# Mixture-of-experts stage: w1 and w3 side by side in the array's columns, and another order of the expert steps

## The chip, the cores and the metric

The kernel runs on one core of a Trainium2 chip. The metric is the device time of one launch in microseconds (us). PE is TensorE's matmul pipe and PEld its weight load, DVE is VectorE, ACT is ScalarE, SP is the engine whose queue issues the weight loads. Line numbers (L1541) are those of the kernel before.

## The reference, cut to what matters

A hybrid layer is followed by a two-layer block. The second layer of that block ends in a mixture of eight experts: 256 tokens of width 1024, each sent to its two best experts, each expert a gated feed-forward of inner width 3584.

```
def moe_swiglu(x, w_router, w1, w3, w2):
    ...
    top_vals, top_idx = lax.top_k(logits, TOP_K)          # TOP_K = 2
    gates = jax.nn.softmax(top_vals, axis=-1)
    ...
    def block_fn(args):
        tok, e = args
        xb = xf[tok]
        return (jax.nn.silu(xb @ w1[e]) * (xb @ w3[e])) @ w2[e]
    ...
h = layer_norm(DEEPNORM_ALPHA * h + f + e, ln2_g[i], ln2_b[i])
```

All is float32. Everything ahead of the experts (some 1000 us) is untouched by the change.

## The kernel before, in words

The experts are sorted at run time by how many tokens they have (`who`), so that "expert 1" below is a rank and not a number of the model. Expert 0 is always the model's first one. Each rank has room for a fixed number of tokens: 64 for 0, 4 and 5, 128 for 2 and 3, 128 + 64 for 1 (its second block has the number `NE`), 32 for 6 and 7. A block of 128 is "wide" and a block of 64 or 32 "narrow". Five more passes for experts that overflow stand in a conditional at the end and are not run on these inputs.

The inner width is cut into NJ = 7 slices of 512, and one slice of one expert is a step: 56 steps, listed in `STEPS`. A step reads six units of 1 MiB: w1 as two units (input rows 0 to 511 and 512 to 1023), w3 as two, w2 as two (output columns 0 to 511 and 512 to 1023). `_moe_order` gives the order of the units: the four of a step's w1 and w3, then the two of w2 of the step before. `prepare` issues a unit's load on SP's queue into the next of a ring of raw buffers (eight of them from step 2 on) and, for ranks in `WIDE`, has ACT cast each half to a high part (`whi`, L302) and DVE subtract to a low part (`wlo`, L303). `rows_unit` runs three units ahead of their use, so these instructions stand in the queues of SP, ACT and DVE ahead of what belongs to the units in use.

`hidden` is the up part of a step (x w1 and x w3). A wide block keeps the tokens transposed and split in two (`xg`) and takes three matmuls for each 128 rows of a unit (`mm3`, L321 to L323, 128 columns of the array). A narrow block (`xn`) takes the raw float32 weights (L1584; each float32 product appears as two instructions) and only 64 or 32 columns of the array; `pair` puts neighbouring k into different column groups, so that two (64) or four (32) of them run side by side, and their partial sums stand in different partitions of one PSUM bank. `turned` transposes such a bank (L1568) and DVE adds the partial sums (L1572). This is done twice for a narrow block in each step: for w1 in the middle of the up part and for w3 in `later`. `later` also applies silu and the product, and for a wide block transposes it (L1553). `down` is the product with w2, for the step before; `passes` puts `later` between its two halves. Ranks in `aside` add each step's product to a tile in SBUF (L1604); the others accumulate in two PSUM banks over all seven steps. After an expert's last step `scaled` and `scatter` (L1626) add its tokens to the residual.

`gather` (L1430 and on) picks a group's tokens by a one-hot matmul, for whole groups of ranks, up to three steps ahead of their first use. `last_sums` and `last_norm` end the kernel after the last step.

The order of the instructions on each engine comes from a scheduler that runs when the kernel is built: it takes the written order as priority and gives buffers to tiles as they come free.

```
STEPS = _steps((0, 0, 0, 4, 0, 4, 0, 4, 0, 4, 0, 4, 4, 4) + (1, 5, 6) * NJ + (2, 7) * NJ + (3,) * NJ)
```

Of the kernel before, what the change touches and what calls it, by code (L numbers as in the profile page):

```python
# [8 lines left out]
F32 = mybir.dt.float32  # L9
# [4 lines left out]
OP = mybir.AluOpType  # L14
# [192 lines left out]

def _moe_order(steps):

    out = []  # L210
    for i in range(len(steps) + 1):
        if i < len(steps):
            out += [(steps[i][0], 6 * steps[i][1] + t) for t in range(4)]
        if i:
            out += [(steps[i - 1][0], 6 * steps[i - 1][1] + t) for t in (4, 5)]
    return out

STEPS = _steps((0, 0, 0, 4, 0, 4, 0, 4, 0, 4, 0, 4, 4, 4) + (1, 5, 6) * NJ + (2, 7) * NJ + (3,) * NJ)  # L220

WIDE = (1, 2, 3)

# [22 lines left out]
class Kern:  # L246
# [925 lines left out]
    def moe(self, l, h, hT, out):  # L1172
# [6 lines left out]
        with ExitStack() as ctx:  # L1179
# [143 lines left out]
            def widen():  # L1323
                rctx.close()
                more = ctx.enter_context(tc.tile_pool(name="more", bufs=1, side="right"))
                self.xgs = [more] * 4
                self.xns = [more] * 3 + self.xns
                self.ohs = [more] * 4 + self.ohs
                self.ya = more
            es = [nc.sync.value_load(who[0:1, i:i + 1], min_val=0, max_val=NE - 1) for i in range(1, NE)]  # L1330
            self.srcs += [(A["wm"][0, u] if e == 0 else self.wsrc(es[e - 1], u), e in WIDE)
# [4 lines left out]
            def rows():  # L1336

                for i in range(2):
                    t = self.ya.tile([P, D], F32, name=f"y{5 + i}")
                    for c in range(2):  # L1340
                        acc = self.bank([P, 4, P], "acc")
                        for k in range(4):
                            at = KD * i + 4 * c + k
                            mm(acc[:, k], self.gb[:, at:at + 1].to_broadcast([P, P]), self.ident, start=True, stop=True)
                        nc.scalar.copy(t[:, 512 * c:512 * c + 512], acc.rearrange("p a b -> p (a b)"))
                    gb.append(t)
                fin.extend(self.ya.tile([P, D], F32, name=n) for n in ("y7", "y8"))
                stats.append(self.mp.tile([P, NT, 2, 6], F32, name="stats"))

            def done(sums):  # L1350
                self.last_norm(r, sums, fin, stats[0], *gb, out)
            self.passes(posp, gatep, STEPS, r, first, [
                {4: [(4, b)]}, {1: [(1, a), (NE, b)], 5: [(5, b)]},
                {6: [(6, q)], 7: [(7, q)]}, {2: [(2, a)]}, {3: [(3, a)]}], (NE, 4, 5, 6, 7), {2: narrow, 3: widen, len(STEPS) - NJ + 2: rows}, done)
            n = nc.values_load(who[0:1, NE + MORE:], min_val=0, max_val=MORE)
            with ExitStack() as some:
                for i in range(MORE):
                    some.enter_context(tc.If(n > i))
                    e = nc.sync.value_load(who[0:1, NE + i:NE + i + 1], min_val=0, max_val=NE - 1)
                    steps = _steps((0,) * NJ)  # L1360
                    self.srcs, self.ready = [(self.wsrc(e, u),) for _, u in _moe_order(steps)], []
                    self.passes(posp, gatep, steps, r, {}, [{0: [(NE + 1 + i, a)]}], done=done)

    def last_norm(self, x, sums, out, st, g, b, dst):

# [47 lines left out]
    def gather(self, gate, group, oh):  # L1413
# [5 lines left out]
        blocks = sum(group.values(), [])  # L1419
        starts = [sum(n for _, n in blocks[:i]) for i in range(len(blocks) + 1)]  # L1420
        width = starts[-1]
        gsl = self.gat.tile([P, 3], F32, name="gsl", bufs=2)
        xs = [tuple(self.turn_of(self.xgs, [P, KD, P], "xg") for _ in range(2)) if n == P else
              (self.turn_of(self.xns, [P, KD, n], "xn", F32),) for _, n in blocks]
        for k in range(0, KD, 2):
# [31 lines left out]
    def passes(self, pos, gate, steps, r, got, groups, aside=(), events={}, done=None):  # L1457

        todo, left, ys = None, None, {}
        groups = list(groups)  # L1460
        for i, step in enumerate(steps + [None]):
            new = None
            if i in events:
                events[i]()

            for e, _ in steps[i:i + (3 if i > 5 else 1)]:
                if e not in got:
                    got.update(self.gather(gate, groups[0], self.one_hot(pos, groups.pop(0))))
            later = None
            if step:  # L1470
                e, j = step
                out, later = self.hidden([b[1] for b in got[e]])
                new = (e, j, out)
            if left:
                self.scatter(left, r)
                left = None
            if not step:
                break
            if todo:
                e, j, gs = todo  # L1480
                if j == 0:
                    ys[e] = [self.ya.tile([P, D], F32, name=f"y{7 if b[0] == 4 else b[0]}") if b[0] in aside else
                             [self.bank([P, 512], "sm") for _ in range(2)] for b in got[e]]
                    ys[e] = [[y[:, :512], y[:, 512:]] if b[0] in aside else y for y, b in zip(ys[e], got[e])]
                here = [b[0] in aside for b in got[e]]
                self.down(ys[e], gs, j, here, (0,))
                later()
                self.down(ys[e], gs, j, here, (1,))
                if j == NJ - 1:
                    left = self.scaled(ys[e], got[e])  # L1490
            else:
                later()
            todo = new
        done(self.last_sums(r, todo, ys, got, aside))
# [26 lines left out]
            scatter(1, parts)  # L1521
        yield outs

    def hidden(self, xs):


        nc, mp = self.nc, self.mp
        hs = [[], []]
        for i in range(2):
            accs = [self.bank([P, 512], "acc") for _ in xs]  # L1530
            for k0 in (0, 4):
                w = self.rows_unit(512)
                for x, acc in list(zip(xs, accs))[::1 if k0 == 0 else -1]:
                    for k in range(4):
                        self.pair(acc, x, k0 + k, w, k, k0 == 0, k0 + 4 == KD, 4)
                if i == 1 and k0 == 0:
                    sums = [self.turned(s, 4, x[0].shape[-1]) if len(x) == 1 else None for x, s in zip(xs, hs[0])]
            for x, acc in zip(xs, accs):
                if len(x) == 1 or i == 0:
                    t = mp.tile([P, 512], F32, name="eg", bufs=3)  # L1540
                    nc.scalar.activation(t, acc, AF.Copy if len(x) == 1 else AF.Silu)  # L1541
                    acc = t
                hs[i].append(acc)
        out = []

        def later():
            for x, s, t, g in zip(xs, *hs, sums):
                if len(x) == 2:
                    gh, gl = (mp.tile([P, 4, P], F32R, name="egs", bufs=4) for _ in range(2))
                    nc.vector.tensor_mul(s, s, t)  # L1550
                    tp = self.bank([P, 4, P], "tp")
                    for k in range(4):
                        t = nc.tensor.transpose(tp[:, k], s[:, k * P:k * P + P], self.ident)  # L1553
                        if k == 0:
                            self.tc.keep_in_program_order(t)
                    self.split(gh, gl, tp)
                    out.append((gh, gl))
                else:
                    nc.scalar.activation(g, g, AF.Silu)
                    nc.vector.tensor_mul(g, g, self.turned(t, 2, x[0].shape[-1]))  # L1560
                    out.append((g,))
        return out, later

    def turned(self, a, bufs, n):

        tp = self.bank([P, 4, P], "tp")
        for k in range(4):
            i = self.nc.tensor.transpose(tp[:, k], a[:, k * P:k * P + P], self.ident)  # L1568
            if k == 0:
                self.tc.keep_in_program_order(i)  # L1570
        g = self.mp.tile([P, 4, n], F32, name=f"g{bufs}", bufs=bufs)
        self.nc.vector.tensor_reduce(g, tp.rearrange("p k (h s) -> p k s h", s=n), axis=AX.X, op=OP.add)  # L1572
        return g

    def pair(self, out, x, kx, w, k, first, last, n):
# [10 lines left out]

    def down(self, ys, gs, j, aside, halves=(0, 1), between={}):
        nc = self.nc
        outs = [[self.ps.tile([P, 512], F32, name=n, bufs=3) for n in ("acc", "sm")] if a else y
                for y, a in zip(ys, aside)]  # L1590
        for c in halves:
            w = self.rows_unit(512)
            for y, g, a in list(zip(outs, gs, aside))[::1 if c == 0 else -1]:
                for k in range(4):
                    self.pair(y[c], g, k, w, k, a or j == 0, a or j == NJ - 1, 4)
                    if k in between:
                        between[k]()
            for y, o, a in zip(ys, outs, aside):
                if not a:
                    continue  # L1600
                if j == 0:
                    nc.scalar.copy(y[c], o[c])
                else:
                    nc.vector.tensor_add(y[c], y[c], o[c])  # L1604
# [45 lines left out]
```

## Time and profile before

| what | value |
|---|---|
| median of 3 runs (lowest, highest) | 1933.09 us (1931.63, 1933.33) |
| the profiled execution: its own time, its span | 1931.92 us, 1930.0 us |
| mean granted TensorE clock | 0.976 |
| PE busy, share of the span | 1824.0 us, 95% |
| PEld busy | 1299.2 us, 67% |
| DVE busy | 1202.9 us, 62% |
| ACT busy | 871.9 us, 45% |
| read from HBM | 512.24 MB, 266 GB/s over the span |

All times below are of that one execution and count from the start of its span. "Busy" of PE is the time in which at least one matmul is under way; matmuls overlap, so a busy PE may still wait between two of them. The expert steps begin at about 990 us and last to the end.

### The profile page before, as it was taken

To read this page: it belongs to the slowest core of one execution; us is meant where nothing else is said; L and a number is where in the kernel's file an instruction comes from. 1 tells how busy PE (TensorE), PEld (TensorE's weight loads), DVE (VectorE), ACT (ScalarE), POOL (GpSimd) and SP (SyncE) were. 2 spreads that over 40 slices of the span, in tenths; PEclk is the share of its full clock that TensorE was granted. 3 is DMA by queue.
4 is the path that set the end of the run, shared out by engine and by line. 5 is a ranking of instruction groups with operands and counts; after the bars stand their busy time and mean duration, and the time that the engine had idled before them with its cause. 6 is when DMAs were issued, how large, how long until landed. Compare 5 with 4: busy or idle time off the path is not lost. (4 is left out here: it accounts for less than half of the span.)

```text
span 1930.0 us, 27247 instructions
## 1 busy us (share of the span) xinstructions
PE 1824.0 (95%) x10410; PEld 1299.2 (67%) x10410; DVE 1202.9 (62%) x2179; ACT 871.9 (45%) x1411; POOL 8.8 (0%) x21
## 2 busy tenths in 40 slices
PE   6999999998998999999799989999999999989996
PEld 6998888897875999787554235444444556656775
DVE  6548899757897655589741114534444476656887
ACT  4656565443463554347311113433223444545674
POOL 0000000000000000000000000000000000000000
PEclk9999999999998999999899999999999999999998
DMA  6543444454534555463459999889999899999982
GB/s 244 194 155 110 153 167 161 170 203 173 209 119 157 186 175 186 176 240 116 196 198 389 421 421 418 353 348 369 364 366 369 343 371 422 421 421 386 381 341 87
DMA packets 82875, 515.19 MB, mean 267 GB/s; under 512 B 8689, under 2 KB 17569, under 8 KB 22961
## 3 DMA queue, kind: packets, MB, share of 16 engines
q1 hardware_dynamic: 69296, 494.57, 66.1%
q10 hardware_dynamic: 13440, 18.80, 3.0%
q8 instruction: 84, 1.38, 0.3%
q14 instruction: 55, 0.44, 0.1%
HBM read 512.24 MB, written 1.10 MB: 266 GB/s over the span
## 5 line engine op out<-in xcount | busy, mean ns | idle before, releaser
L303 DVE TENSOR_TENSOR wlo<-raw,whi 128x1024 fp32r<-128x1024 f32 x490 | 582.2, 1220 | 157.4 <-ACT whi L302 156.4
L302 ACT CAST whi<-raw 128x1024 fp32r<-128x1024 f32 x490 | 494.9, 1048 | 167.8 <-PE acc L322 68.9
L1584 PE MATMUL acc<-raw,xn 128*64 128x512 f32 (+1 forms) x1344 | 274.1, 606 | 8.6 <-DMA raw<-in_wm 8.6
L1572 DVE TENSOR_REDUCE g<-tp 128x256 f32<-128x512 f32 (+1 forms) x84 | 58.0, 690 | 268.4 <-PE tp L1568 268.4
L1541 ACT ACTIVATE eg<-acc 128x512 f32<-128x512 f32 x105 | 62.0, 597 | 286.0 <-PE acc L1584 215.6
L1584 PEld LDWEIGHTS acc<-raw,xn 128*64 128x64 f32 (+1 forms) x1344 | 75.4, 129 | 153.0 <-issue 126.3
L321 PE MATMUL acc<-uhi,whi 128*128 128x272 f32 (+1 forms) x576 | 168.4, 293 | 1.4 <-DVE rs_t L379 1.4
L322 PE MATMUL acc<-ulo,whi 128*128 128x272 f32 (+1 forms) x576 | 167.9, 292 | 0.0
L323 PE MATMUL acc<-uhi,wlo 128*128 128x272 f32 (+1 forms) x576 | 166.5, 289 | 0.0
L321 PE MATMUL acc<-hhi,whi 128*128 128x256 f32 x544 | 152.6, 280 | 0.0
L322 PE MATMUL acc<-hlo,whi 128*128 128x256 f32 x544 | 152.3, 280 | 0.0
L323 PE MATMUL acc<-hhi,wlo 128*128 128x256 f32 x544 | 151.8, 279 | 0.0
L321 PE MATMUL acc<-whi,xg 128*128 128x512 f32 x336 | 135.9, 405 | 4.4 <-ACT whi L302 4.4
L322 PE MATMUL acc<-wlo,xg 128*128 128x512 f32 x336 | 135.3, 403 | 0.8 <-DVE wlo L303 0.8
L323 PE MATMUL acc<-whi,xg 128*128 128x512 f32 x336 | 133.0, 396 | 0.0
L321 PEld LDWEIGHTS acc<-uhi,whi 128*128 128x128 f32 x576 | 109.7, 191 | 4.6 <-issue 2.7
L322 PEld LDWEIGHTS acc<-ulo,whi 128*128 128x128 f32 x576 | 109.6, 190 | 1.4 <-issue 1.0
L323 PEld LDWEIGHTS acc<-uhi,wlo 128*128 128x128 f32 x576 | 109.6, 190 | 1.3 <-issue 1.1
L1021 DVE SCALAR_TENSOR_TENSOR cv<-u,cols,cv 128x256 f32<-128x256 f32 x240 | 102.2, 481 | 2.1 <-ACT cv L1019 1.3
L321 PEld LDWEIGHTS acc<-hhi,whi 128*128 128x128 f32 x544 | 102.3, 188 | 0.1
L322 PEld LDWEIGHTS acc<-hlo,whi 128*128 128x128 f32 x544 | 102.1, 188 | 0.1
L323 PEld LDWEIGHTS acc<-hhi,wlo 128*128 128x128 f32 x544 | 101.8, 187 | 0.0
(516 smaller groups left out, 3085.1 us busy)
## 6 DMA issues: line engine op xcount, KB each, us to landing
raw<-in_wm SPq DMA_DIRECT2D x336, 1024.0 KB, 9.7
raw<-in_ws SPq DMA_DIRECT2D x131, 1024.0 KB, 4.8
row<-in_rows ACTq DMA_DIRECT2D x9, 512.0 KB, 4.6
seg<-racs ACTq DMA_DIRECT2D x8, 512.0 KB, 3.7
rb<-in_rpb ACTq DMA_DIRECT2D x8, 512.0 KB, 3.9
ck<-rnck ACTq DMA_DIRECT2D x4, 544.0 KB, 5.4
x<-in_x SPq DMA_DIRECT2D x2, 512.0 KB, 5.3
gn<-in_rows ACTq DMA_DIRECT2D x4, 256.0 KB, 3.3
```

The lines of the kernel that those rows point to most:

```text
L302: nc.scalar.copy(hi, x)
L303: nc.vector.tensor_sub(lo, x, hi.bitcast(F32))
L321: nc.tensor.matmul(out, lhi, rhi, start=start, stop=False)
L322: nc.tensor.matmul(out, lhi, rlo, start=False, stop=False)
L323: nc.tensor.matmul(out, llo, rhi, start=False, stop=stop)
L1021: nc.vector.scalar_tensor_tensor(cv[:, m], u[:, m, t:t + T], w, cv[:, m], op0=OP.mult, op1=OP.add)
L1541: nc.scalar.activation(t, acc, AF.Copy if len(x) == 1 else AF.Silu)
L1572: self.nc.vector.tensor_reduce(g, tp.rearrange("p k (h s) -> p k s h", s=n), axis=AX.X, op=OP.add)
L1584: self.nc.tensor.matmul(out[h:h + s], x[0][:, kx], w.raw[:, k], start=first and k < m, stop=last and k >= n - m)
```

## The change: what it does

`TURNS` names the ranks with a narrow block. For them the order of the four up units becomes w1 first half, w3 first half, w1 second half, w3 second half, and `products` takes both units of a half at once: w1's product goes to partitions 0 to 63 of one bank and w3's to 64 to 127 (for 32 tokens, two pieces of 32 each). One ACT copy, one set of four transposes and `gated` then serve both: for 64 tokens silu and product read the transposed bank directly, for 32 DVE adds the two pieces of each first. Ranks 2 and 3 keep their order of units; silu of the w1 product is now issued after the w3 product.

`STEPS` becomes: 0, 0, 0, 4, 0, 4, 0, 4, then seven pairs of rank 2 with 0, 4 and (the last) 5, then seven times (1, 6, 7), then six pairs (3, 5) and a last 3. Each rank still has seven steps. `EARLY` gathers the group of ranks 1 and 5 at step 13 and that of 6 and 7 at step 17. Rank 2 now accumulates in SBUF. `rows` (the rows of the last norm's gain and bias) is two steps earlier.

```diff
-            out += [(steps[i][0], 6 * steps[i][1] + t) for t in range(4)]
+            out += [(steps[i][0], 6 * steps[i][1] + t) for t in ((0, 2, 1, 3) if steps[i][0] in TURNS else range(4))]
...
-STEPS = _steps((0, 0, 0, 4, 0, 4, 0, 4, 0, 4, 0, 4, 4, 4) + (1, 5, 6) * NJ + (2, 7) * NJ + (3,) * NJ)
+TURNS = (0, 1, 4, 5, 6, 7)
+STEPS = _steps((0, 0, 0, 4, 0, 4, 0, 4, 2, 0, 2, 4, 2, 0) + (2, 4) * 3 + (2, 5) + (1, 6, 7) * NJ + (3, 5) * (NJ - 1) + (3,))
+EARLY = (13, 17)
...
-                {4: [(4, b)]}, {1: [(1, a), (NE, b)], 5: [(5, b)]},
-                {6: [(6, q)], 7: [(7, q)]}, {2: [(2, a)]}, {3: [(3, a)]}], (NE, 4, 5, 6, 7), {2: narrow, 3: widen, len(STEPS) - NJ + 2: rows}, done)
+                {4: [(4, b)]}, {2: [(2, a)]}, {1: [(1, a), (NE, b)], 5: [(5, b)]},
+                {6: [(6, q)], 7: [(7, q)]}, {3: [(3, a)]}], (NE, 2, 4, 5, 6, 7), {2: narrow, 3: widen, len(STEPS) - NJ: rows}, done)
...
+            if len(steps) > NJ and i in EARLY:
+                got.update(self.gather(gate, groups[0], self.one_hot(pos, groups.pop(0))))
...
+    def hidden(self, xs, turns):
+        if turns:
+            hs = self.products(xs)
+        else:
+            accs = []
+            for i in range(2):
+                accs.append(self.bank([P, 512], "acc"))
+                for k0 in (0, 4):
+                    w = self.rows_unit(512)
                     for k in range(4):
+                        self.pair(accs[i], xs[0], k0 + k, w, k, k0 == 0, k0 + 4 == KD, 4)
+            hs = [accs]
+        for h in hs:
+            t = mp.tile([P, 512], F32, name="eg", bufs=3)
+            nc.scalar.activation(t, h[0], AF.Copy if len(h) == 1 else AF.Silu)
+            h[0] = t
...
+    def products(self, xs):
+        hs = [[self.bank([P, 512], "acc") for _ in x] for x in xs]
+        for k0 in (0, 4):
+            ws = [self.rows_unit(512) for _ in range(2)]
+            for x, h in list(zip(xs, hs))[::-1 if k0 == 0 else 1]:
+                if len(x) == 2:
+                    for w, acc in zip(ws, h):
+                        for k in range(4):
+                            self.pair(acc, x, k0 + k, w, k, k0 == 0, k0 + 4 == KD, 4)
+                    continue
+                n = x[0].shape[-1]
+                m = P // n // 2
+                for k in range(0, 4, m):
+                    for i, w in enumerate(ws):
+                        for q in range(m):
+                            at = P // 2 * i + n * q
+                            self.nc.tensor.matmul(h[0][at:at + n], x[0][:, k0 + k + q], w.raw[:, k + q],
+                                                  start=k0 + k == 0, stop=k0 + k + m == KD)
+        return hs
+
+    def gated(self, tp, n):
+        g = self.mp.tile([P, 4, n], F32, name="g4", bufs=4)
+        if n == 64:
+            s = self.mp.tile([P, 4, n], F32, name="g2", bufs=2)
+            nc.scalar.activation(s, tp[:, :, :n], AF.Silu)
+            nc.vector.tensor_mul(g, s, tp[:, :, n:])
+        else:
+            s = self.mp.tile([P, 8, n], F32, name="g2", bufs=2)
+            nc.vector.tensor_reduce(s, tp.rearrange("p k (b h s) -> p (k b) s h", b=2, s=n), axis=AX.X, op=OP.add)
+            s = s.rearrange("p (k b) s -> p k b s", b=2)
+            nc.scalar.activation(s[:, :, 0], s[:, :, 0], AF.Silu)
+            nc.vector.tensor_mul(g, s[:, :, 0], s[:, :, 1])
...
-        outs = [[self.ps.tile([P, 512], F32, name=n, bufs=3) for n in ("acc", "sm")] if a else y
+        outs = [[self.ps.tile([P, 512], F32, name=n, bufs=3) for n in ("sm", "acc")] if a else y
...
-            for y, g, a in list(zip(outs, gs, aside))[::1 if c == 0 else -1]:
+            for y, g, a in list(zip(outs, gs, aside))[::-1 if c == 0 else 1]:
```

## Rows read from the trace of the kernel before

**Rows 1.** Busy time by stage (start:end, length, each engine's busy us, PEclk, DMA share, GB/s):
```profile
990.00:1051.00 61.00, 61.00 (x294) 24.61 (x294) 10.43 (x27) 10.13 (x20) 0.00 (x0) 0.91 0.90 355
1051.00:1192.00 141.00, 130.59 (x702) 51.78 (x701) 33.53 (x66) 26.11 (x63) 0.00 (x0) 1.00 1.01 421
1192.00:1580.00 388.00, 386.22 (x1864) 186.72 (x1862) 186.59 (x237) 140.65 (x194) 0.00 (x0) 1.00 0.92 362
1580.00:1787.00 207.00, 188.25 (x967) 123.50 (x959) 131.86 (x142) 105.59 (x133) 0.00 (x0) 0.94 0.99 409
1787.00:1913.00 126.00, 122.49 (x550) 95.78 (x550) 105.49 (x104) 84.63 (x97) 0.00 (x0) 0.99 0.75 295
1913.00:1930.00 17.00, 1.20 (x4) 0.32 (x3) 9.74 (x28) 1.74 (x3) 0.00 (x0) 0.59 0.18 67
```

**Rows 2.** The weight loads of the experts, on the page (KB each, us to landing):
```profile
raw<-in_wm SPq DMA_DIRECT2D x336, 1024.0 KB, 9.7
```

**Rows 3.** The loads' own line from 1003 us (ns min/median/max, first and last start):
```profile
L295 SPq DMA_DIRECT2D raw<-in_wm x323: 327/333/1002, 1003.5 to 1885.2; - x162
...
DMA to landing us min/median/max: 4.7/9.8/19.0
```

**Rows 4.** Busy time of one narrow step, of two (1,5,6) rounds, of three wide steps:
```profile
1044.70:1056.50 11.80, 11.80 (x60) 4.12 (x58) 1.81 (x3) 2.20 (x4) 0.00 (x0) 1.00 1.01 422
1260.20:1362.90 102.70, 102.70 (x489) 47.48 (x488) 46.47 (x56) 35.81 (x48) 0.00 (x0) 1.00 0.92 367
1829.50:1881.70 52.20, 52.20 (x230) 41.40 (x229) 43.26 (x41) 36.19 (x41) 0.00 (x0) 1.00 0.90 342
```

**Rows 5.** Chain of waits inside one (1,5,6) round (start us, us to the next):
```profile
1311.67 1.87 PE acc L1584 x8
1313.54 0.59 PE tp L1568 x4
...
1315.99 0.43 PE acc L321
1316.42 0.23 PE acc L322
...
1322.00 5.30 PE acc L1584 x24
...
1340.91 2.71 PE acc L1584 x24
```

**Rows 6.** Chain of waits around a gather of 128 tokens (L1430):
```profile
1527.57 3.72 PE acc L1430 x32
...
1532.13 2.29 PE acc L1584 x9
```

**Rows 7.** Groups by line from 1000 us (busy us, mean ns, idle before):
```profile
L303 DVE TENSOR_TENSOR wlo<-raw,whi 128x1024 fp32r<-128x1024 f32 x252 | 292.8, 1220 | 60.1 <-ACT whi L302 59.8
L302 ACT CAST whi<-raw 128x1024 fp32r<-128x1024 f32 x252 | 246.5, 1047 | 18.7 <-PE acc L323 10.4 <-DMA raw<-in_wm 4.3 <-PE sm L323 3.6
...
L1626 PE MATMUL acc<-yh,ohT 128*128 128x512 f32 x32 | 13.3, 422 | 0.6 <-DVE hb L1628 0.4
...
L1626 PE MATMUL acc<-yl,ohT 128*128 128x512 f32 x32 | 12.6, 397 | 0.0
...
L1344 PE MATMUL acc<-cst,wr 128*128 128x128 f32 x32 | 3.9, 275 | 0.0
```

**Rows 8.** The last matmul, in the order of time:
```profile
1913.85 0.40 PE L1507 MATMUL sm<-yl,ohT 128*128 128x512 f32 x1
```

**Rows 9.** Chain of waits in one (2,7) round, across a wait for a load:
```profile
1604.95 8.78 DMA raw<-in_wm
...
1617.11 0.43 PE sm L323
```

**Rows 10.** Busy time and granted clock around that wait:
```profile
1610.00:1630.00 20.00, 17.59 (x82) 12.06 (x75) 13.02 (x13) 11.25 (x13) 0.00 (x0) 0.83 1.01 421
```

**Rows 11.** Waits from 960 us: who waited for whom, us in total, times, longest:
```profile
PEld sm L321 <- ACT whi L302: 20.7, 12, 3.4
```

More of the change, by code (lines that the diff above doesn't have):

```diff
@@ L1327, in widen @@
                 self.xns = [more] * 3 + self.xns
-                self.ohs = [more] * 4 + self.ohs
+                self.ohs = [more] * 5 + self.ohs
                 self.ya = more
@@ L1338, in rows @@
                 for i in range(2):
-                    t = self.ya.tile([P, D], F32, name=f"y{5 + i}")
+                    t = self.ya.tile([P, D], F32, name=f"y{6 + i}")
                     for c in range(2):
@@ L1346, in rows @@
                     gb.append(t)
-                fin.extend(self.ya.tile([P, D], F32, name=n) for n in ("y7", "y8"))
+                fin.extend([self.ya.tile([P, D], F32, name="y8"), self.turn_of(self.xgs, [P, D], "xg", F32)])
                 stats.append(self.mp.tile([P, NT, 2, 6], F32, name="stats"))
@@ L1359, in moe @@
                     e = nc.sync.value_load(who[0:1, NE + i:NE + i + 1], min_val=0, max_val=NE - 1)
-                    steps = _steps((0,) * NJ)
+                    steps = _steps((2,) * NJ)
                     self.srcs, self.ready = [(self.wsrc(e, u),) for _, u in _moe_order(steps)], []
-                    self.passes(posp, gatep, steps, r, {}, [{0: [(NE + 1 + i, a)]}], done=done)
+                    self.passes(posp, gatep, steps, r, {}, [{2: [(NE + 1 + i, a)]}], done=done)
     def last_norm(self, x, sums, out, st, g, b, dst):
@@ L1421, in gather @@
         width = starts[-1]
-        gsl = self.gat.tile([P, 3], F32, name="gsl", bufs=2)
+        gsl = self.gat.tile([P, 3], F32, name="gsl", bufs=5)
         xs = [tuple(self.turn_of(self.xgs, [P, KD, P], "xg") for _ in range(2)) if n == P else
@@ L1471, in passes @@
                 e, j = step
-                out, later = self.hidden([b[1] for b in got[e]])
+                out, later = self.hidden([b[1] for b in got[e]], e in TURNS)
                 new = (e, j, out)
@@ L1481, in passes @@
                 if j == 0:
-                    ys[e] = [self.ya.tile([P, D], F32, name=f"y{7 if b[0] == 4 else b[0]}") if b[0] in aside else
+                    ys[e] = [self.ya.tile([P, D], F32, name="y%d" % {4: 7, 2: 6}.get(b[0], b[0])) if b[0] in aside else
                              [self.bank([P, 512], "sm") for _ in range(2)] for b in got[e]]
@@ L1522, in last_sums @@
         yield outs
-    def hidden(self, xs):
+    def hidden(self, xs, turns):
         nc, mp = self.nc, self.mp
[L1528 to L1533, printed above, removed]
-                    for k in range(4):
[L1535 to L1543, printed above, removed]
+        if turns:
[6 more added lines that the diff above has]
+                    w = self.rows_unit(512)
+                    for k in range(4):
+                        self.pair(accs[i], xs[0], k0 + k, w, k, k0 == 0, k0 + 4 == KD, 4)
[4 more added lines that the diff above has]
+            h[0] = t
@@ L1544, in hidden @@
         out = []
         def later():
-            for x, s, t, g in zip(xs, *hs, sums):
-                if len(x) == 2:
-                    gh, gl = (mp.tile([P, 4, P], F32R, name="egs", bufs=4) for _ in range(2))
[L1550 to L1555, printed above, removed]
+            for x, h in zip(xs, hs):
+                if len(h) == 2:
+                    nc.vector.tensor_mul(h[0], *h)
+                tp = self.bank([P, 4, P], "tp")
+                for k in range(4):
+                    i = nc.tensor.transpose(tp[:, k], h[0][:, k * P:k * P + P], self.ident)
+                    if k == 0:
+                        self.tc.keep_in_program_order(i)
+                if len(h) == 2:
+                    gh, gl = (mp.tile([P, 4, P], F32R, name="egs", bufs=4) for _ in range(2))
@@ L1558, in later @@
                 else:
-                    nc.scalar.activation(g, g, AF.Silu)
-                    nc.vector.tensor_mul(g, g, self.turned(t, 2, x[0].shape[-1]))
-                    out.append((g,))
+                    out.append((self.gated(tp, x[0].shape[-1]),))
         return out, later
[L1564 to L1572, printed above, removed]
+    def products(self, xs):
[5 more added lines that the diff above has]
+                    for w, acc in zip(ws, h):
+                        for k in range(4):
+                            self.pair(acc, x, k0 + k, w, k, k0 == 0, k0 + 4 == KD, 4)
[9 more added lines that the diff above has]
+        return hs
@@ new lines, in gated @@
+    def gated(self, tp, n):
+        nc = self.nc
+        g = self.mp.tile([P, 4, n], F32, name="g4", bufs=4)
[9 more added lines that the diff above has]
+            nc.vector.tensor_mul(g, s[:, :, 0], s[:, :, 1])
```

## The prediction

> **What bounds the kernel now.** I read the busy time by stage first, because the page's 95% for PE mixes stages with different limits. Until 1051 us and again from 1192 to 1580 PE is busy throughout, while the loads run below the 421 GB/s of the stage between (355 and 362); from 1051 to 1192 and from 1580 to 1787 the loads run at 421 and 409 GB/s and PE has idle time; from 1787 on PE is busy and the loads fall to 295 [rows 1]. So the expert stage is bound in turn by its loads (narrow steps, and pairs of rank 2 with 7) and by PE (rounds of 1, 5, 6 and lone wide steps of 3). While one is the bound, the other loses time that it can't use later, since at most eight units can wait in raw buffers.
>
> **The floor of the loads.** A load is 1024 KB [rows 2], 1.0486 MB, and at 421 GB/s [rows 1] takes 2.49 us; a step's six take 14.9. From 1051 to 1913 the four stages moved 421x141 + 362x388 + 409x207 + 295x126 = 321.7 MB [rows 1], which at 421 GB/s is 764 us. Without a gap the last load would land at 1815. It was issued at 1885.2 and a load takes at least 4.7 us [rows 3], so it landed at about 1890: 75 us of the channel lie idle. The change moves the same 336 units, in another order; SP issues them as before and has nothing else to do.
>
> **What a step costs PE.** A wide step alone: 52.20/3 = 17.4 us. A 64-token block alone: 11.8. A round (1, 5, 6): 51.35 [rows 4]. A 32-token block, by its pieces: 24 matmuls in 2.71, its other 24 in the same, and two sets of transposes at 0.59 each, 6.6 [rows 5]. Against 14.9 us of loads a wide step is long and a narrow one short. Before, fourteen short steps run in a row (11.8 against 14.9 each), then come rounds of 51.35 against 18x2.49 = 44.8, then pairs (2, 7) of 17.4 + 6.6 = 24 against 29.9, then lone wide steps.
>
> **Part 1, shared columns.** A narrow block keeps 48 matmuls in each step and as many column groups side by side. One of its two sets of four transposes goes (0.59) and so does one break in a run of matmuls: eight alone take 1.87, eight of a run of 24 take 5.30/3 = 1.77 [rows 5]. That is 0.7 us for each of 42 block-steps, 29 us of PE in all. An ACT copy and one or two DVE additions go too; they are worth nothing in themselves, since DVE is busy for 43.26 of 52.20 us even in the lone wide steps [rows 4], where its load is highest. A pair of column groups fed from two different units isn't in the trace. Nearest row: two groups fed from two slices of one unit, 0.22 us a matmul (5.30/24). From above, 0.43, one that has a drain before it; from below, 0.11, the 32-column pace of 2.71/24 [rows 5]. I take 0.22: same columns, same rows, same length.
>
> **Part 2, wide next to narrow.** A wide matmul right behind narrow ones takes 0.43 us, within its run 0.23 [rows 5]: 0.2 for each change. The Trainium skill says in "TensorEngine Tiling (Array Packing)", section Key Properties, that changing the tiling mode, not just the tile, drains TensorE: a rule against this order, which has narrow beside wide in 48 of 56 steps. By the row, four changes in each of 13 pairs cost 10 us in all, and a sum without the drain would come out by so much earlier; I keep it in.
>
> A pair (2, 0), (2, 4) or (3, 5) thus costs PE 17.4 + 11.1 + 0.8 = 29.3 us at least. What it waits for beyond that the trace doesn't show. From above: the round (1, 5, 6) costs 51.35 - 17.4 - 2x11.8 - 6.6 = 3.75 more than its pieces, drains included, or 2.5 in two thirds of it: 31.0. From below nothing is gained, 29.3. I take 29.7, nearer the low end, because within the steps of a pair wide and narrow don't alternate as in rank 1's up part. That is just under the 29.9 of its loads.
>
> A round (1, 6, 7): 51.35, less 11.8 - 6.6 for a 32-token block in place of 5's, less 3x0.7, is 44.05; I take 44, between 46.2 (sharing gives nothing) and 43 (the two changes saved in rank 1's up part, and two waits). Its loads are 44.8. Within a round the two don't keep pace: rank 1's four up units take PE some 18 us (10 of loads), the next six 7 (15), its two down units 10 (5), the last six 6 (15). The loads thus have to be ahead by about 8 us, three to four units, and with two units in use and two in flight the eight buffers just hold that.
>
> **The sum.** The narrow step of rows 4 is step 4, so step 5 begins at 1056.5. From there on PE: steps 5 to 7, 3x11.1 = 33.3; seven pairs, 207.9; seven rounds, 308; six pairs and a wide step, 195.6. Four gathers from the first use of rank 2 on: 1532.13 - 1527.57 = 4.56 each [rows 6], 18.2, and 4 for the smaller blocks' own transposes. All 64 scatter matmuls at 0.233, 14.9, and 3.9 for `rows` [rows 7]. Together 785.8, so the last matmul begins at 1842.3. In the kernel before it begins at 1913.85 [rows 8], 16.15 ahead of the end at 1930.0: the end is 1858.5. The loads by themselves: the last lands at 1815, its two halves are cast and subtracted (one cast of 1.05 and two subtractions of 1.22 are on the path [rows 7]), six matmuls follow (1.4), and the closing part is 18 to 19 us by the rows of before (from some two us ahead of its last matmul): 1838. PE is later by 20 us, so PE sets the end by a little and both are nearly full. The profiled execution's own time is 1.92 above its span, and the median of three is 1.17 above that: 1858.5 + 3.1 = **1861.6**, 3.7% less than before.
>
> At nothing I cost these. The early gathers are counted above, wherever they stand. Rank 2's products are added in SBUF: 14 more DVE additions in seven pairs of 29.9 us, in which DVE has 14.4 for a wide step [rows 4] and these few. The swap of the two banks in `down`: both come free a step earlier. Silu of ranks 2 and 3, issued after both products: its bank is ready half an up part earlier and behind it in ACT's queue stand narrow units, which need no cast. If a cast is in its way, that is 1.05 us [rows 7] in each of 14 steps, 15 us.
>
> **The rivals.**
> *The loads set the end.* If pairs cost 29.3 and rounds 43, PE's sum falls by 12 and the ends meet: 1841 to 1848. For it speaks that the loads held 421 GB/s over whole stages; against it the gathers and scatters, 41 us that PE has beside the steps.
>
> *PE's clock falls.* In the (2,7) rounds PE waits 8.78 us for a load, the granted clock of that stretch is 0.83 in the mean, which is some time at 1.2 GHz, and matmuls behind the wait take 0.43 us in place of 0.23 [rows 9, 10]. Twelve of them cost 2.4 us more. Once in each of 20 pairs and rounds that is 48, in half of them 24: 1885. Against it: a PE with 0.2 us to spare in a pair and 0.8 in a round has little to wait for, and in the rounds of before, with PE full, the clock was 1.00 [rows 4]. The Trainium skill has the rule in "TensorE: Matmul & The Clock Gate", section What's actually happening: the default state is throttled, and activity releases the throttle. The trace agrees where PE waits.
>
> *The copies behind the casts (slower).* Before, half of a narrow block's transposes came early, in the third unit; now all come after the up part and wait for one ACT copy. ACT takes its queue in order, and ahead of that copy stand the casts of up to three later units, which wait for their loads. Where wide units follow a narrow up part (7 + 14 + 6 = 27 places) PE would stand until they have landed: 20.7 us in 12 such waits before, the longest 3.4 [rows 11]. At that longest in all 27 it is 92 us and the time 1953, slower than before; it decides from 2.8 us a place. Against it: the mean was 1.7, which would give 46 and 1908, and these waits came while the loads ran full, so that they cost nothing.
>
> *It doesn't do what it says.* If column groups of two units don't run side by side, a matmul takes 0.43 and 896 of them (28 block-steps of 32) add 188 us. Against it: the array sees the same columns.
>
> **How the numbers follow.** The forecast, 1850 to 1875, 58%; the loads' floor, below 1850, 17%; the clock or half of the copies, 1875 to 1925, 18%; the copies at full price or no overlap, 5%; the gains cancelled by mishaps, within 0.2%, 2%. From no change a measurement of this kernel can tell about 0.2%, 4 us. Faster 0.93, same 0.02, slower 0.05. The range: below, the loads' floor with 3 us less, 1838; above, rounds at 46.2 (+15) and pairs at 31.0 (+17), 1893.
>
> **What would show it.** Right: 42 copies and 42 sets of narrow transposes less; loads at 400 GB/s or more from 1051 to 1800; pairs of about 30 us and rounds of about 45; the last load issued before 1830. Wrong: a gap in the loads beyond a few us in the rounds (the eight buffers don't suffice), PE idle behind ACT's copies while the loads are not full, a granted clock under 0.95 in the pairs, narrow matmuls slower than 0.22.

## The result: 0.5% slower, and the profile after

The changed kernel takes 1943.5 us (median of five runs, 1940.3 to 1946.5), the kernel before 1933.3 beside it: a ratio of 1.0053, with a 95% interval of 1.0037 to 1.0069. The forecast was 1861.6, 3.7% faster, with a range of 1838 to 1893. It was wrong, by 82 us and in the sign. Line numbers from here on are those of the kernel that a row comes from (L1588, L1590 and L1591 are one and the same line).

The span is 1941.6 us. First the stages, in the columns of [rows 1]; from 1192 on they are the pairs of rank 2, the rounds (1, 6, 7), the pairs (3, 5) and the close:

```profile
990.00:1051.00 61.00, 60.90 (x314) 25.40 (x314) 4.64 (x17) 8.57 (x18) 0.00 (x0) 0.95 0.92 376
1051.00:1192.00 141.00, 131.64 (x625) 70.49 (x621) 53.62 (x71) 51.28 (x83) 0.00 (x0) 1.00 0.99 410
1192.00:1341.00 149.00, 137.64 (x638) 83.86 (x639) 85.34 (x102) 60.45 (x80) 0.00 (x0) 0.95 0.90 355
1341.00:1688.00 347.00, 324.48 (x1704) 160.62 (x1702) 158.22 (x188) 124.15 (x168) 0.00 (x0) 0.98 0.93 380
1688.00:1912.00 224.00, 207.97 (x885) 126.58 (x885) 120.39 (x125) 93.61 (x113) 0.00 (x0) 0.96 0.88 348
1912.00:1942.00 30.00, 12.00 (x44) 7.69 (x44) 20.73 (x43) 6.77 (x10) 0.00 (x0) 0.76 0.11 38
```

Before, one of the two was full in nearly every stage [rows 1]. Now, from 1192 to 1912, neither is: PE is idle for 11, 23 and 16 us, and the loads run at 355, 380 and 348 GB/s where 421 is to be had. The last load, issued at 1885.2 before [rows 3], is issued at 1892.0, so none of the 75 us of idle channel came back:

```profile
L301 SPq DMA_DIRECT2D raw<-in_wm x324: 327/333/1154, 1001.4 to 1892.0; - x162
```

One pair of rank 2 with a narrow rank, with no gather or scatter in it, from one wide product to the next, and one round (1, 6, 7), where [rows 4] have a wide step, a narrow step and two rounds (1, 5, 6):

```profile
1284.60:1317.62 33.02, 30.61 (x130) 18.52 (x132) 18.36 (x19) 13.49 (x16) 0.00 (x0) 0.95 0.96 384
1552.74:1600.37 47.63, 44.33 (x234) 21.54 (x236) 21.60 (x25) 15.74 (x20) 0.00 (x0) 0.96 0.97 399
```

The pair was forecast at 29.7 and takes 33.0; the round was forecast at 44 and takes 47.6. Of the seven pairs without gather or scatter three take 33.0, three 31.5 (the part on the clock below says why) and the first, which waits about 1 us for a load besides, 32.7.

**Where a pair loses time.** The chain of waits through it (columns as in [rows 5]; L1588 is the narrow up part, L327 to L329 the three products of a wide matmul, `sm` the wide down part):

```profile
1288.88 6.92 PE acc L1588 x32
1295.80 0.02 issue
1295.82 0.02 ACT eg L1549
...
1296.32 1.04 ACT whi L308
1297.36 0.02 issue
1297.39 1.24 DVE wlo L309
1298.62 0.04 issue
1298.67 0.50 PE sm L328
1299.16 0.23 PE sm L329
1299.39 0.41 PE sm L327
1299.80 0.43 PE sm L328
```

The narrow up part runs as forecast: 6.92/32 = 0.216 us a matmul, so column groups fed from two units do run side by side. Behind it the chain leaves PE for the narrow copy, a cast and a subtraction of the next wide down unit. Then the matmuls go on at 0.43 us, while the granted clock of the pair is 0.95 in the mean. Now ScalarE's queue over the same stretch (start, us, instruction; in brackets its idle time before and who ended it):

```profile
1279.39 1.99 ACT L308 CAST whi<-raw 128x1024 fp32r<-128x1024 f32 x2
1287.05 0.59 ACT L364 CAST egs<-tp 128x512 fp32r<-128x512 f32 x1 [5.67 <-PE tp L1559]
1295.82 0.60 ACT L1549 ACTIVATE eg<-acc 128x512 f32<-128x512 f32 x1 [8.18 <-PE acc L1588]
1296.32 3.87 ACT L308 CAST whi<-raw 128x1024 fp32r<-128x1024 f32 x4
```

ScalarE does nothing for 8.18 us: the next instruction in its queue is the narrow copy (L1549), which waits for the end of the narrow up part. Behind it stand four casts, those of the two wide down units. Their loads were issued at 1279.4 and 1282.9 and landed at 1285.6 and 1288.1, 10.7 and 8.3 us before the first of these casts began. TensorE needs these casts at the very moment at which the narrow up part ends, and that is when ScalarE begins them.

The waits from 990 us say how often (those of before are [rows 11], and `wlo` behind `whi`, 59.8 us there [rows 7]):

```profile
ACT eg L1549 <- PE acc L1588: 267.0, 42, 10.3
DVE wlo L309 <- ACT whi L308: 182.6, 72, 14.1
...
PEld sm L327 <- ACT whi L308: 38.5, 20, 2.5
...
PE sm L327 <- ACT whi L308: 21.4, 13, 1.7
```

The last row has 13 waits: one in each of the 13 pairs. Behind it TensorE does one matmul and waits 0.76 us more, for the subtraction.

**Where a round loses time.** The waits of SP, which issues the loads, over the rounds:

```profile
SPq L301 <- PE acc L1588: 149.0, 49, 13.3
```

A load waits for a raw buffer, and the buffer for the last instruction that reads it, which for a narrow block is a matmul. Rank 1's up units are read by its narrow block NE too, directly from the raw buffer. In the second half of that up part the narrow block comes last, so that buffers which the wide block gave up long ago (it reads the casts) stay taken. The longest stop is 13.3 us. PE pays later in the round, when it waits for a load that was issued behind such a stop, after eight others, and took 14.47 us to land, in its chain of waits:

```profile
1423.27 14.47 DMA raw<-in_wm
1437.77 1.05 ACT whi L308
1438.84 1.24 DVE wlo L309
...
1440.12 0.50 PE acc L328
```

### The profile page after: what moved, and what is told of

The parts are those of the page before. It is cut to its first block, busy times and chain, and to the rows that moved or that the text cites. A ratio compares the mean times of both kernels' runs of the same rounds, so it can differ in the third digit from the quotient of the medians.

```text
span 1941.6 us, 26683 instructions
## 1 busy us (share of the span) xinstructions
PE 1809.2 (93%) x10242; PEld 1291.8 (67%) x10242; DVE 1167.9 (60%) x2121; ACT 848.0 (44%) x1371; POOL 8.8 (0%) x21
## 4 chain that ended last, share of the span: by engine, by line
PE 78%; DVE 11%; DMA 6%; ACT 3%; issue 2%; DVEq 0%; ACTq 0%; SPq 0%
PE acc L328 14%; PE acc L327 14%; PE acc L329 14%; PE acc L1588 12%; DMA raw<-in_wm 6%; DVE wlo L309 4%; PE sm L1617 3%; DVE cv L1027 2%; PE sm L328 2%; PE sm L329 2%; PE acc L1617 2%; PE sm L327 2%; ACT whi L308 2%; PE tp L1559 1%; PE acc L1436 1%
## 5 line engine op out<-in xcount | busy, mean ns | idle before, releaser
L1588 PE MATMUL acc<-raw,xn 128*64 128x512 f32 (+1 forms) x1344 | 277.2, 606 | 8.6 <-DMA raw<-in_wm 8.5
L1588 PEld LDWEIGHTS acc<-raw,xn 128*64 128x64 f32 (+1 forms) x1344 | 82.0, 130 | 176.3 <-issue 158.2
L1549 ACT ACTIVATE eg<-acc 128x512 f32<-128x512 f32 x63 | 37.6, 598 | 331.4 <-PE acc L1588 267.0
L327 PE MATMUL acc<-uhi,whi 128*128 128x272 f32 (+1 forms) x576 | 168.5, 293 | 1.2 <-DVE rs_t L385 1.2
L329 PE MATMUL acc<-uhi,wlo 128*128 128x272 f32 (+1 forms) x576 | 166.8, 290 | 0.0
L327 PE MATMUL acc<-hhi,whi 128*128 128x256 f32 x544 | 152.6, 280 | 0.0
L329 PE MATMUL acc<-hhi,wlo 128*128 128x256 f32 x544 | 152.2, 280 | 0.0
L327 PE MATMUL acc<-whi,xg 128*128 128x512 f32 x336 | 136.1, 405 | 4.7 <-ACT whi L308 4.7
L329 PE MATMUL acc<-whi,xg 128*128 128x512 f32 x336 | 135.2, 402 | 0.0
L327 PEld LDWEIGHTS acc<-uhi,whi 128*128 128x128 f32 x576 | 110.0, 191 | 4.5 <-issue 2.3
L329 PEld LDWEIGHTS acc<-uhi,wlo 128*128 128x128 f32 x576 | 109.9, 191 | 1.3 <-issue 1.1
L327 PEld LDWEIGHTS acc<-hhi,whi 128*128 128x128 f32 x544 | 101.9, 187 | 0.1
L329 PEld LDWEIGHTS acc<-hhi,wlo 128*128 128x128 f32 x544 | 102.0, 188 | 0.0
L1617 PE MATMUL sm<-raw,g 128*64 128x512 f32 (+1 forms) x392 | 84.1, 602 | 1.5 <-DMA raw<-in_wm 1.4
```

The costliest lines, as they stand in the source:

```text
L327: nc.tensor.matmul(out, lhi, rhi, start=start, stop=False)
L329: nc.tensor.matmul(out, llo, rhi, start=False, stop=stop)
L1549: nc.scalar.activation(t, h[0], AF.Copy if len(h) == 1 else AF.Silu)
L1588: self.nc.tensor.matmul(h[0][at:at + n], x[0][:, k0 + k + q], w.raw[:, k + q], start=k0 + k == 0, stop=k0 + k + m == KD)
L1617: self.nc.tensor.matmul(out[h:h + s], x[0][:, kx], w.raw[:, k], start=first and k < m, stop=last and k >= n - m)
```

## The experiments

Ratios are to the kernel before, run beside each on the same chip; the changed kernel is at 1.0053 on this scale. The first four take the two waits away one at a time, and take the change apart.

**The narrow copies behind the casts.** The copy is kept, on its engine, behind all that the program wrote before it, so that the casts of the next three units go first:

```diff
-            nc.scalar.activation(t, h[0], AF.Copy if len(h) == 1 else AF.Silu)
+            i = nc.scalar.activation(t, h[0], AF.Copy if len(h) == 1 else AF.Silu)
+            if len(h) == 1:
+                self.tc.keep_in_program_order(i)
```

> The only change: ScalarE's copy of a narrow block's up result is kept behind the casts written before it, so that up to six casts of later units run ahead of it; the matmuls are the same. Theory A (in ScalarE's queue the casts of a wide step's down units stand behind a copy that waits for the narrow up part, though their units landed some 10 us before): the 33.0 us of a clean pair (2, x) fall to 30 or 31, thirteen pairs give back 25 to 40 us, the rounds little: 1903 to 1920, and the idle time of ScalarE before that copy (267 us in 42) falls below 150. Theory B (the raw buffers are too few, or the loads are the limit, and the casts only show it): the copy now waits for casts that wait for loads, and the narrow transposes come later by that: 1940 to 1965.

Measured: 1906.1 us, ratio 0.9875 (0.9857 to 0.9893): 34 us less than the changed kernel, theory A; ScalarE's idle time before the copy falls from 267 to 103 us. First ScalarE's queue in the same pair, then a pair and a round in the columns of [rows 1]:

```profile
1275.59 1.99 ACT L308 CAST whi<-raw 128x1024 fp32r<-128x1024 f32 x2 [0.34 <-DMA raw<-in_wm]
1278.08 1.99 ACT L308 CAST whi<-raw 128x1024 fp32r<-128x1024 f32 x2 [0.49 <-DMA raw<-in_wm]
1282.08 1.99 ACT L308 CAST whi<-raw 128x1024 fp32r<-128x1024 f32 x2 [2.01 <-DMA raw<-in_wm]
1283.97 0.59 ACT L1549 ACTIVATE eg<-acc 128x512 f32<-128x512 f32 x1
```

```profile
1272.22:1301.30 29.08, 28.98 (x130) 17.35 (x132) 18.27 (x20) 13.70 (x16) 0.00 (x0) 1.00 1.01 419
1484.69:1532.60 47.91, 45.04 (x234) 21.54 (x236) 21.60 (x25) 15.75 (x20) 0.00 (x0) 0.96 0.95 394
```

The casts run as their loads land, under the narrow up part; the copy comes at 1283.97, just after that part. The pair falls from 33.02 to 29.08, TensorE is busy in all but 0.1 us of it at clock 1.00, and the loads run at 419 GB/s. The round stays at 47.9, as theory A has it. Theory B named a real price: ScalarE's casts now wait 121.7 us for loads, in 37 waits of up to 14.9 us; but in such a pair TensorE doesn't pay it. The chain behind the narrow up part shows what became of the 0.43 us matmuls:

```profile
1276.50 6.87 PE acc L1590 x32
1283.37 0.43 PE sm L327
1283.80 0.23 PE sm L328
```

One matmul at 0.43 is left, the change from narrow to wide of [rows 5].

**Narrow first in both halves.** This moves rank 1's narrow block ahead in the second half of its up part, and nothing else:

```diff
-            for x, h in list(zip(xs, hs))[::-1 if k0 == 0 else 1]:
+            for x, h in list(zip(xs, hs))[::-1]:
```

> The only change: in the second half of an up part with a wide and a narrow block (rank 1 alone) the narrow block's matmuls come first, as in the first half, so that the raw buffers of these units are free once they are cast. Theory A2 (in a round the raw buffers of rank 1's last up units are held until the narrow part, no load is issued for some 14 us, and TensorE waits for loads in the next step): the stretch without an issue falls by 7 us or more, a round goes from 48 to 45 or 46, seven of them give 14 to 21 us: 1922 to 1930. Theory B2 (rounds too are late because casts stand behind narrow copies): less than 5 us: 1939 to 1944, one more change between wide and narrow in each of 7 steps being 7 x 0.4 us.

Measured: 1929.0 us, ratio 0.9995 (0.9982 to 1.0008), 11 us less than the changed kernel: theory A2, somewhat below its size. A round, and SP's waits over the rounds:

```profile
1507.69:1552.41 44.72, 42.94 (x236) 20.83 (x239) 21.52 (x25) 15.64 (x20) 0.00 (x0) 1.00 1.01 421
```

```profile
SPq L301 <- PE acc L1588: 107.3, 50, 7.7
```

The longest stop falls from 13.3 to 7.7 us (by 5.6, where 7 or more were expected), and the round from 47.6 to 44.7, its loads at 421 GB/s.

**The new order alone, and the shared columns alone.** The first has the steps and gathers of the change with `hidden`, `down` and the unit order of before; the second has the shared columns with the steps of before (and five `gsl` buffers, so that its gathers have room).

> The new order of steps and of gathers with the narrow up part of before (w1 and w3 in columns of their own, half of a narrow block's transposes after its third unit, banks and unit order as before). If the order of steps is what costs (wide casts behind narrow copies in every pair): 1945 to 1985, slower than the changed kernel by about the 0.7 us x 42 = 29 us that shared columns save TensorE, less what is hidden. If the shared columns are what costs (one copy and all transposes after the up part): 1890 to 1925, faster than the changed kernel, near the forecast plus 29.

> The shared columns (with their copies, products, unit order and additions) in the order of steps and of gathers of before. If the columns do on TensorE what they save (0.7 us in each of 42 block-steps) and the order is what costs: in the rounds (1, 5, 6), where TensorE was the bound, 3 x 0.7 us in each of 7, and in the pairs: 1905 to 1925. If the columns themselves cost (the narrow copy waits for the whole up part, and the casts of the next wide units stand behind it in 14 more places): 1940 to 1960.

Measured: the order alone 1936.7 us, ratio 1.0035 (1.0020 to 1.0049); the columns alone 1918.1, ratio 0.9932 (0.9917 to 0.9948). The order is what costs: 0.35% without the shared columns and 1.2% with them. The columns give 0.7%, 13 us, in the old order; in the new one they give nothing that the ratios can tell (1.0053 with them, 1.0035 without). The first guess of the order's price, 1945 or more, was too high. The trace of the order alone tells the two waits apart. Its clean pairs have the wait of the changed kernel (1.63 us for the cast and 0.75 for the subtraction in the one from 1281.91, which takes 33.72), so that one comes with the order. Its rounds of 46.1 us have TensorE busy throughout and no stop of the loads above 7.1 us, so the stop of 13.3 came with `products`, where the narrow block reads both units of the second half last.

**Both edits together, with eight raw buffers and with seven.**

> Both edits together on the changed kernel: the narrow copies behind the casts, and the narrow block of rank 1 first in both halves. If the two waits are separate (pairs wait for casts, rounds for loads): a clean pair 29 to 30 us, a round of ranks 1, 6 and 7 44 to 45, so that the 37 and the 14 us which they gave alone add up: 1888 to 1897. If the loads take over as the bound as soon as one is gone, or the casts in the rounds now stand in the way: 1900 to 1908, no more than the copies alone.

> As the kernel with both edits, but seven raw buffers for the loads in place of eight in the expert stage. If the number of buffers is what still limits (a buffer is one unit of 2.49 us of loads): the rounds grow by about 2.5 us each and the pairs by 0 to 2: 1905 to 1935. If eight are more than it needs: within 4 us of the kernel with both edits.

Measured: with both 1889.9 us, ratio 0.9785 (0.9772 to 0.9797): the gains add up, and a little more (34 and 11 give 46; it is 52 below the changed kernel). This kernel beats both others, by 2.15% and 2.7%. With seven buffers 1909.3, ratio 0.9896 (0.9876 to 0.9916): 21 us of it are gone. With both edits, a pair and a round, then SP's waits over the rounds, then the loads' own line:

```profile
1271.65:1300.75 29.10, 28.99 (x130) 17.33 (x132) 18.26 (x19) 13.71 (x16) 0.00 (x0) 1.00 1.01 421
1482.46:1527.42 44.96, 43.57 (x236) 21.14 (x238) 21.51 (x25) 15.54 (x20) 0.00 (x0) 1.00 1.01 421
```

```profile
SPq L301 <- PE acc L1590: 82.5, 42, 7.0
```

```profile
L301 SPq DMA_DIRECT2D raw<-in_wm x324: 327/333/1257, 1000.3 to 1838.8; - x162
```

Pair and round now hold 421 GB/s, and the pair has TensorE full as well: the state that the forecast described. With seven buffers clean pairs take 29.1 to 30.1 and the rounds, from one wide product to the next, 46 to 49 us after a first of 54 (with eight: 45 after a first of 50); it is in the rounds that eight are just enough.

**The old order with both edits.**

> The order of steps and gathers of before with the shared columns and with both edits (the narrow copies behind the casts, narrow first in both halves). If the new order is worth what the forecast gave it (75 us of idle channel recovered by wide next to narrow) once the waits are gone: 1900 to 1915, 10 us or more slower than the new order with both edits. If the old order was as good, and only the columns bring something: 1885 to 1898, level with it.

Measured: 1921.7 us, ratio 0.9948 (0.9936 to 0.9960), above both ranges and no better than the columns alone (0.9932). Wide next to narrow is therefore worth 1.6%, 31 us, where both orders have both edits, and 1.5%, 28 us, against the columns alone; without the edits the same order costs time.

**The narrow copies on VectorE.** In place of the pin, VectorE makes the copies, with narrow first as before:

```diff
+            if len(h) == 1:
+                nc.vector.tensor_copy(t, h[0])
+            else:
+                nc.scalar.activation(t, h[0], AF.Silu)
```

> As the kernel with both edits, but the narrow copies are not pinned: VectorE makes them, so that ScalarE's casts stand behind none of them. VectorE's queue has the subtractions of the same units in place of the casts, and by the order in which the program is laid out they can stand behind the copy as the casts did. If it is the queue of ScalarE alone that counts: 1885 to 1897. If the subtractions now wait in the casts' place (a wide matmul needs both halves): 1905 to 1930.

Measured: 1908.7 us, ratio 0.9890 (0.9872 to 0.9908), the second case: the wait has moved to the other queue. VectorE, then TensorE, in a pair:

```profile
1289.56 0.69 DVE L1550 COPY eg<-acc 128x512 f32<-128x512 f32 x1 [6.21 <-PE acc L1591]
1290.17 4.62 DVE L309 TENSOR_TENSOR wlo<-raw,whi 128x1024 fp32r<-128x1024 f32 x4
```

```profile
1289.42 0.49 PE L327 MATMUL sm<-whi,egs 128*128 128x512 f32 x1
1291.44 0.50 PE L328 MATMUL sm<-wlo,egs 128*128 128x512 f32 x1 [1.53 <-DVE wlo L309]
```

VectorE stands for 6.21 us before the copy with four subtractions behind it. The first wide matmul, which needs the cast alone, starts at once; the second waits 1.53 us for its subtraction. The pair takes 30.5 us, between 29.1 and 33.0.

**How many casts have to go first.** Units prepared two, or one, ahead in place of three (`self.ahead = 2`, `= 1`), with both edits, so that four, or two, casts stand ahead of the copy.

> As the kernel with both edits, but units are prepared two ahead in place of three, so that four casts stand ahead of the pinned narrow copy in place of six: those of the two down units of the wide step, while the next wide step's first up unit is cast behind it. If what counts is that the down units are cast ahead of the copy: within 5 us of the 1890 with six. If it is the general lead of the casts over the matmuls: part of the 37 us comes back, 1900 or more.

> As the kernel with both edits, but units are prepared one ahead: two casts stand ahead of the narrow copy, those of the first down unit; the second's two follow the copy. The first down unit's twelve matmuls take 2.8 us, the copy, a cast of 1.05 and a subtraction of 1.22 about as long, so that a pair should lose 0 to 1.5 us: 1890 to 1910. If it comes out as slow as without the pin (1925 or more), the first down unit was not what the pairs waited for.

Measured: 1891.7 us, ratio 0.9804 (0.9791 to 0.9817), and 1890.0, ratio 0.9791 (0.9773 to 0.9810), against 0.9785 with six. The two casts of the first down unit are enough; the second unit's follow the copy and are ready while the first unit's matmuls run. What counts is not the lead of the casts over the matmuls, but that the one unit that TensorE wants next does not stand behind the copy.

**The kernel before, with its narrow copies pinned.**

> The kernel before, with its narrow copies (two for a block) kept behind the casts written before them and nothing else. If the kernel before paid the same wait already (its narrow copies stood ahead of casts too, in its rounds and in the pairs of ranks 2 and 7): 1900 to 1925. If its order kept wide units away from it: within 5 us of before, 1927 to 1937, or slower, because the narrow blocks' first transposes now wait for casts.

Measured: 1938.5 us, ratio 1.0044 (1.0031 to 1.0057), slower. The pin takes waits away here too (20.7 us in 12 [rows 11]; 12.3 in 5 with the pin), but no time comes back, and it has a price: a round (1, 5, 6) goes from 51.4 to 51.9 us. The wait itself was there before the change and cost next to nothing; the next part shows it.

## Why the prediction was wrong

**The step that failed: the pair.** "I take 29.7", with bounds of 29.3 and 31.0. TensorE's work in a pair was right: 29.1 is what it takes once the casts are in time. What failed is the term for waiting beyond that work, 0.4 us and at most 1.7. It was taken from a round (1, 5, 6), as if the queue of ScalarE did the same to a pair. In the new pair the order that the build gave ScalarE puts the copy of the narrow block ahead of the casts of the wide down units. TensorE waits 1.66 us for the cast and 0.76 for the subtraction, and a clean pair takes 31.5 us, or 33.0 where the clock falls too: both are above the bound. From one wide product to the next the thirteen pairs are 1.8 to 4.3 us shorter with the copies pinned, 42 us in all; the time falls by 34, and by 41 (0.9995 to 0.9785) when the rounds are mended as well.

**The rival had the queue right and the direction the wrong way round.** "The copies behind the casts" was the slower rival, which "decides from 2.8 us a place": the right engine, the right queue and nearly the right price, but with TensorE's narrow transposes waiting for casts that wait for loads. In truth the casts waited for the copy. The waits that it was priced by, [rows 11], were of this kind already: in nine of the twelve the cast began as soon as a narrow copy ahead of it in the queue ended. ScalarE, then TensorE, in a pair (2, 7) of the kernel before:

```profile
1643.28 0.60 ACT L1541 ACTIVATE eg<-acc 128x512 f32<-128x512 f32 x1
1643.77 7.81 ACT L302 CAST whi<-raw 128x1024 fp32r<-128x1024 f32 x8
1644.86 0.51 PE L321 MATMUL sm<-whi,egs 128*128 128x512 f32 x1 [1.65 <-ACT whi L302]
```

The load of the first cast had landed at 1641.09, and TensorE waits 1.65 us, as in the new pairs. The rival was set aside because these waits "cost nothing". That held there, where the loads ran at 421 GB/s and set the length of the pair; it did not hold in the new pairs, where the work and the loads are nearly even. The order in which the rival feared the two is the remedy: with it ScalarE waited 121.7 us for loads, and TensorE was idle for 0.1 us of a clean pair.

**The round: "the eight buffers just hold that".** The number was right: seven cost 21 us, eight hold 421 GB/s. But the count had "two units in use" as if they came free one after the other. In the second half of rank 1's up part both were held until the narrow block had run, and no load was issued for 13.3 us at the longest. The forecast was 44 and 44.8 for the loads; it measured 47.6, and 44.7 to 45.0 with narrow first.

**Shared columns: right in TensorE's work, small in time.** The pace was right (0.216 us a matmul, forecast 0.22), and so was the saving: in the old order TensorE's busy time falls from 1824.0 to 1797.0 us, 27 where 29 were forecast, and a round (1, 5, 6) from 51.4 to 49.3, three times 0.7. Of that the time shows 13 us, about what the seven rounds give, where TensorE was the bound. In the new order, with the waits in place, it shows none.

**PE's clock.** This rival came, not by itself but as a part of the wait. The row that it was read from was misread: the 8.78 us of [rows 9] are a load's time from issue to landing, while PE stood for 1.65 and 0.76 us there, which is the wait above. In the clean pair shown, eight matmuls behind the waits go at 0.41 to 0.43 us in place of 0.23, about 1.6 of the 3.9 us lost there; the waits are the rest. In that stretch the granted clock is 0.59 in the mean, most of it at the lower level, 1.2 GHz; behind it the clock is back at 1.00:

```profile
1298.67:1302.87 4.20, 4.20 (x11) 3.26 (x12) 3.35 (x3) 1.52 (x2) 0.00 (x0) 0.59 1.01 425
1303.23:1306.00 2.77, 2.77 (x15) 2.27 (x14) 2.09 (x3) 2.49 (x4) 0.00 (x0) 1.00 1.01 423
```

With the copies pinned the whole pair is at 1.00. Without the pin the clock falls behind these waits in six of the thirteen pairs, and in seven it stays. A clean pair in which it stays:

```profile
1843.08:1874.56 31.48, 29.07 (x130) 17.42 (x132) 17.07 (x17) 13.51 (x16) 0.00 (x0) 1.00 0.99 389
```

**What is left.** The two edits give back 52 of the 82 us. With both the profiled execution takes 1890.3 us, 29 above the forecast. A clean pair is then 0.6 us shorter than forecast and a round 0.9 longer, which nearly cancels over thirteen pairs and seven rounds. Of the 29, the trace shows a pair with a gather at 35.7 and one with a scatter at 32.9, so 6.6 and 3.8 us more than a clean pair, where the forecast had 4.56 + 1 and 1.86. If the other gathers and scatters are like these, that is 4 x 1 + 8 x 1.9 = 19 us, an estimate. No run took the rest apart; the first round, at 50 us in place of 45, is a part of it. The last load is issued at 1838.8; the forecast wanted it before 1830.

**The marks.** Of the signs that the forecast named for being right, the 42 copies and 42 sets of transposes less came (105 copies to 63, and 168 matmul instructions fewer on the page); the loads, the pairs and rounds and the last load did not. Of those for being wrong, three came: a gap in the loads in the rounds, PE idle behind ScalarE's copies while the loads were not full, and, just, the clock, which stands at the 0.95 named in the pairs in which it falls. The fourth, a narrow matmul slower than 0.22, did not.

## What to carry to other kernels

When steps change places, write down each engine's queue across the new seam, and for each instruction that waits on TensorE ask whether TensorE's next input stands behind it: that can cost both engines their overlap though neither is full. A bound taken from a round of before holds only as long as the order of every queue in it is the same. A wait that costs nothing in the rows of before, because another engine or the loads set the pace there, has to be priced at its length where they don't. A buffer that two consumers read is free after the later one, so let the consumer that reads the raw data go first.

## What the runs showed of the hardware that was not expected

Waits of the same length, at the same place in the program, cost TensorE's clock in some pairs and leave it alone in others. In the changed kernel a wide down part begins with a wait of 1.62 to 1.66 us, one matmul and a wait of 0.75 to 0.77. Behind that the clock falls to the lower level in six of the thirteen pairs, and in seven it stays at 1.00. Where it stays, the clean pairs take 31.5 us, about the 2.42 us of the waits more than the 29.1 with the copies pinned; where it falls, they take some 1.6 us more again, 33.0. With the copies on VectorE the part begins with one matmul and a wait of 1.44 to 1.53 us. The matmuls behind it come at 0.23 us, and the clock stays at 1.00 behind all thirteen of these waits; one of the pairs:

```profile
1278.34:1308.83 30.49, 28.96 (x130) 17.35 (x132) 18.76 (x20) 12.91 (x15) 0.00 (x0) 1.00 1.00 409
```

What sets the six pairs apart from the seven no run shows.
